# One of four weight-block sums in the downward stages formed by an adding transfer from GpSimd

## The chip, the cores and the metric

The kernel runs on one core of a Trainium2 chip. The metric is the device time of one execution in microseconds. The time before is the median of three runs. One more execution was taken by the hardware profiler; all rows of a profile come from such a single execution.

## The reference

One layer of a streaming encoder on `x` (1024 tokens of 1024 values, float32), with weights in float32. Two SwiGLU feed-forward blocks stand around a mixer of two attentions:

```python
h = modulate(x, norm_g[l, 0], mod[:, 0, 0], mod[:, 0, 1])
x = x + 0.5 * mod[:, 0, 2][:, None, :] * swiglu(h, ffn1_w1[l], ffn1_w3[l], ffn1_w2[l])
h = modulate(x, norm_g[l, 1], mod[:, 1, 0], mod[:, 1, 1])
y = hybrid_mixer(h, w_in[l], ...)
x = x + mod[:, 1, 2][:, None, :] * y
h = modulate(x, norm_g[l, 2], mod[:, 2, 0], mod[:, 2, 1])
x = x + 0.5 * mod[:, 2, 2][:, None, :] * swiglu(h, ffn2_w1[l], ffn2_w3[l], ffn2_w2[l])
```

`swiglu(h, w1, w3, w2)` is `(silu(h @ w1) * (h @ w3)) @ w2` with 2816 inner columns. The last product, by `w2`, is a downward stage; there are two of them, one in each feed-forward block.

## The kernel before

**Precision.** Each float32 operand of a product is split into a high half (`wh`, ScalarE's copy into a rounded format) and a low half (`wl`, VectorE's `src - wh`). A product is three matmuls: high by high, high by low, low by high (`mm3`).

**The downward stage** (class `Down`). `w2` has 22 blocks of 128 rows by 1024 columns. The stage is a 2 x 2 block product, made with seven products instead of eight (Strassen's scheme in Winograd's form). For each of the 11 pairs `q`, the four 128 x 512 blocks of the weight are `a11` and `a12` (block `q`, left and right half) and `a21` and `a22` (block `q + 11`, left and right half). Four sums of blocks are formed, each by one VectorE operation for each `q`: `s3` (`a11 = a11 - a21`), `s2` (`s2 = a22 - a11`), `s1` (`a21 = a21 + a22`) and `s4` (`a12 = a12 - s2`). `ORDER` names the seven products: `a11`, then `a12`, `s2`, the new `a11`, `a22`, the new `a21` and the new `a12`, each by its combination of the hidden values (`g`, which the upward stage has written to `d_g` in HBM). A product `p` runs over the 11 values of `q`; a step (`p`, `q`) splits one weight block and one `g` tile and issues 12 matmuls into four PSUM banks. After the 11 steps, `out` adds the four banks to the output tiles `xc` (and to `u`).

**Where the work waits.** The split tiles `wh` and `wl` come from a ring of 8 each (class `Halves`), so the splits of at most four steps are in being at a time. Raw tiles (`a`, `g`, `xc` and others) come from pools of 128 x 512 tiles. SyncE issues all loads and stores, in one queue; `Down.loads` asks for the tiles of a step six steps ahead.

**The order** is not that of the code. Class `Plan` collects the operations of a long stretch as tasks and places them by a list schedule: it has a guess of the length of each operation (`length`), of when a result can be read (`end`), of a transfer on the wire (`wire`), and of a port that VectorE and GpSimd share (`t.port`). Of the tasks that are ready on each engine it takes the earliest, within a window of 200. It then issues all in that order, and every engine executes its own list in order. Line 358 of `before.py` issues all planned operations, so nearly all rows of the profile carry L358, and the tiles' names tell them apart: `a<-a` is `s3` or `s1`, `s<-a` is `s2`, `a<-a,s` is `s4`, `wl<-a,wh` a low half of a weight block.

**Around it.** GpSimd does little: in the first stage the sums of squares (`nacc`) and some low halves (`wl<-...` of other shapes), in the second nothing. In the first stage the loads for the downward stage start at 443.0 us while the last upward products run; its own matmuls run from about 479 to 699 us. In the second stage the loads start at 2003.6 us, and the kernel ends at 2266.0 us.

Of the kernel before, what the change touches and what calls it, by code (L numbers as in the profile page):

```python
# [16 lines left out]
ALU = mybir.AluOpType  # L17
# [8 lines left out]
H = 512  # L26
# [29 lines left out]
class View:  # L56
# [53 lines left out]
    def real(self):  # L110
        t = self.tile.real()
        for name, a, kw in self.ops:
            t = t[a[0]] if name == "__getitem__" else getattr(t, name)(*a, **kw)
        return t
# [48 lines left out]
class Plan:  # L163
# [18 lines left out]
    def take(self, engine, op, a, kw):  # L182
        if not self.on:
            return getattr(getattr(self.tc.nc, engine), op)(*map(real, a), **{n: real(v) for n, v in kw.items()})
        t = Task(len(self.tasks), engine, op, a, kw)
        t.rank = t.i + self.behind
        self.tasks.append(t)
        writes = [v for v in (a[0], kw.get("accum_out")) if isinstance(v, View)]
        reads = [v for v in list(a[1:]) + [w for n, w in kw.items() if n != "accum_out"] if isinstance(v, View)]
        before = set()  # L190
        for views, write in ((reads, False), (writes, True)):
            for v in views:
                r = v.region()
                for r2, j, w2 in v.tile.log:
                    if (write or w2) and j != t.i and all(p < q2 and p2 < q for (p, q), (p2, q2) in zip(r, r2)):
                        before.add(j)
        for views, write in ((reads, False), (writes, True)):
            for v in views:
                if write and not v.ops:
                    v.tile.log = []  # L200
                v.tile.log.append((v.region(), t.i, write))
        t.ready = max([getattr(v.tile, "written", 0.0) for v in reads] + [0.0])
        tiles = {id(v.tile): v.tile for v in reads + writes + self.wanted}
        self.wanted = []
        for x in tiles.values():
            if x.t is None and x.first is None:
                t.new.append(x)
                x.first = t.i
            elif x.t is None:
                before.add(x.first)  # L210
            x.uses += 1
        t.tiles = list(tiles.values())
        t.written = [v.tile for v in writes]
        for j in before:
            self.tasks[j].after.append(t)
        t.left = len(before)
        out = writes[0] if writes else a[0]
        shape = list(out.shape)
        t.n = int(np.prod(shape[1:]))
        if op == "tensor_reduce":  # L220
            t.n = int(np.prod(a[1].shape[1:]))
        t.bytes = 4 * int(np.prod(shape))
        t.port = engine in ("vector", "gpsimd") and "accum_out" not in kw and not any(
            v.tile.pool.space == PSUM for v in reads + writes)
        if engine == "tensor":
            m = a[2] if op == "matmul" else a[1]
            t.exact = m.tile.dt in (F32R, BF16) or any(o[0] == "bitcast" and F32R in o[1] for o in m.ops)
# [18 lines left out]
    def length(self, t, e):  # L246
        if e == "tensor":
            if t.exact:
                return max(0.08, t.n / 2250.0)
            if t.op == "transpose":  # L250
                return t.n / 860.0
            return max(0.24, t.n / 500.0)
        more = "accum_out" in t.kw
        if e == "scalar":
            return 0.1 + t.n / 1200.0 + (0.3 if more else 0.12 if any(isinstance(t.kw.get(x), View) for x in ("bias", "scale")) else 0.0)
        if e == "vector":
            if t.op == "tensor_tensor_scan":
                return 0.1 + t.n / 450.0
            return max(0.2, 0.08 + t.n / 960.0 + (0.18 if more else 0.06 if t.op == "scalar_tensor_tensor" else 0.0))
        if e == "gpsimd":  # L260
            return 0.1 + t.n / (900.0 if t.op == "tensor_scalar" else 440.0)
        return 0.35

    def flush(self, keep=()):
# [8 lines left out]
        def release(t):  # L273
            insort(waiting[t.engine], t, key=lambda u: u.rank)
# [10 lines left out]
        def slot(t):  # L285

            when, need = 0.0, {}
            for x in t.new:
                if x.kw.get("tag"):
                    need.setdefault(x.key, []).append(x)  # L290
            if need and t.rank > low + self.window:
                return None
            for s, xs in need.items():
                if xs[0].kw["bufs"] == 1 and news[s][0] != t.i:
                    return None
                got = sorted(self.slots(xs[0]))
                if len(got) < len(xs) + (0 if news[s][0] == t.i else min(self.spare, xs[0].kw["bufs"] // 4)):
                    return None
                when = max(when, got[len(xs) - 1][0])
            return when  # L300

        todo = sorted(tasks, key=lambda t: t.rank)
        while len(order) < len(tasks):
            best = None
            while todo[0].placed:
                todo.pop(0)
            low = todo[0].rank
            for e in self.ENGINES:
                w = waiting[e][:60]
                pick, ahead = None, 0.0  # L310
                for t in w:
                    room = slot(t) if t.new else 0.0
                    if room is None:
                        continue
                    s = max(t.ready, room, free[e])
                    if t.port:
                        s = max(s, self.port["gpsimd" if e == "vector" else "vector"])
                    if pick is None or s < pick[0] - 0.05:
                        pick = (s, t, e)
                if pick and (best is None or pick[0] < best[0]):  # L320
                    best = pick
            assert best, "no task can be placed: " + str([(t.engine, t.op, [x.kw for x in t.new]) for w in waiting.values() for t in w][:8])
            s, t, e = best
            d = self.length(t, e)
            end = s + d + 0.12
            if t.port:
                self.port[e] = s + d
            free[e] = s + d
            if e == "sync":
                self.wire = max(self.wire, s + 1.3) + t.bytes / 345e3  # L330
                end = self.wire + 0.7
                free[e] = max(free[e], self.wire - 5.0)
            t.placed = True
            order.append((s, len(order), t, e, d))
            waiting[e].remove(t)
            for x in t.new:
                if x.kw.get("tag"):
                    news[x.key].remove(t.i)
                    x.slot = min(self.slots(x))
                    self.slots(x).remove(x.slot)  # L340
                    x.slot = x.slot[1]
            for x in t.written:
                x.written = max(getattr(x, "written", 0.0), end)
            for x in t.tiles:
                x.uses -= 1
                x.end = max(getattr(x, "end", 0.0), end)
                if not x.uses and x.slot is not None:
                    self.slots(x).append((x.end, x.slot))
                    self.kept.pop(id(x), None)
            for u in t.after:  # L350
                u.left -= 1
                u.ready = max(u.ready, s + d if u.engine == e and e != "sync" else end)
                if not u.left:
                    release(u)
# [152 lines left out]
def t512(k, dt=F32, name="t", home="c"):  # L507

    p, tag, n = k.homes[home]
    return p.tile([128, H], dt, tag=tag, name=name, bufs=n)  # L510
# [824 lines left out]
PAIRS = NF // 2  # L1335
# [232 lines left out]
class Down:  # L1568
# [34 lines left out]
    def sum(self, n, q):  # L1603
        a, nc = {m: t[q] for m, t in self.a.items()}, self.k.nc
        if n == "s3":
            self.any.tensor_sub(a["a11"], a["a11"], a["a21"])
        elif n == "s2":
            t = self.a["s2"][q] = t512(self.k, name="s2")
            self.any.tensor_sub(t, a["a22"], a["a11"])
        elif n == "s1":  # L1610
            self.any.tensor_add(a["a21"], a["a21"], a["a22"])
        elif n == "s4":
            self.any.tensor_sub(a["a12"], a["a12"], a["s2"])

# [668 lines left out]
```

## Time and profile before

| what | value |
|---|---|
| median of 3 runs | 2268.83 us (2267.1 to 2270.32) |
| the profiled execution | 2267.75 us, of which span 2266.0 us |
| mean granted TensorE clock | 0.986 |
| TensorE (PE) busy | 2179.2 us, 96% |
| VectorE (DVE) busy | 1803.8 us, 80% |
| ScalarE (ACT) busy | 1102.1 us, 49% |
| GpSimd (POOL) busy | 296.2 us, 13% |
| DMA, SyncE's queue | 313.89 MB, 41.5% of the span of 16 engines |

Times in the profile are microseconds from the start of the span. A row of a timeline gives start, length, engine, line, operation, result and operands; in brackets stands how long the engine was idle before it and what ended that. A row of a table of groups gives the number of operations and min/median/max of their length in nanoseconds. A row of waits gives the sum, the number of times and the longest.

### The profile page before, as it was taken

The numbers are of one execution on the slowest core, as the hardware profiler recorded it, in microseconds if no ns is written. First come the engines' busy times: TensorE is split into PE (matmuls) and PEld (weight loads), VectorE is DVE, ScalarE is ACT, GpSimd is POOL, SyncE is SP. The second block draws the span as 40 slices with busy tenths as digits, with TensorE's granted clock in tenths as the row PEclk, the third lists the DMA queues.
The fourth block names the chain that finished last, engine by engine and source line by source line (L and its number), as shares of the span: only waits on it lengthen the run. The fifth ranks groups of instructions, "written<-read, shape, count | busy, mean of one in ns | idle before, by whom it ended". The sixth has DMA issues, their size and how long they took to land.

```text
span 2266.0 us, 31234 instructions
## 1 busy us (share of the span) xinstructions
PE 2179.2 (96%) x10508; PEld 1801.7 (80%) x10508; DVE 1803.8 (80%) x3377; ACT 1102.1 (49%) x1996; POOL 296.2 (13%) x269
## 2 busy tenths in 40 slices
PE   7999999999997999998999999799999999999999
PEld 5777888788886989996778787687888888888887
DVE  7998987879685488888688877668898877769765
ACT  5432232344463476787687777423443333334443
POOL 0000000000042113223555433000000000000000
PEclk9999999999998999999999999999999999999999
DMA  9234454495323313333333210767223442258520
GB/s 331 85 113 163 166 173 130 157 355 199 89 92 130 99 49 126 123 120 125 110 106 101 66 44 20 272 227 263 96 80 127 135 132 96 93 186 313 166 77 38
DMA packets 187421, 315.89 MB, mean 139 GB/s; under 512 B 27366, under 2 KB 51942, under 8 KB 187260
## 3 DMA queue, kind: packets, MB, share of 16 engines
q1 hardware_dynamic: 187260, 313.89, 41.5%
q8 instruction: 83, 1.36, 0.3%
q14 instruction: 78, 0.64, 0.1%
HBM read 237.53 MB, written 76.28 MB: 138 GB/s over the span
## 4 chain that ended last, share of the span: by engine, by line
PE 46%; DVE 2%; ACT 2%; DMA 2%; issue 1%; SPq 0%; ACTq 0%; DVEq 0%; POOL 0%
PE b L358 35%; PE py L358 6%; PE pt L358 3%; PE p L358 2%; DMA wr<-in_w_g 1%; ACT pth L358 0%; DVE macc L358 0%; ACT pr L358 0%; DVE ptl L358 0%; ACT kst L358 0%; DMA h<-d_y 0%; DVE qs L358 0%; ACT yt L358 0%; DMA xb<-d_x 0%; DVE kst L358 0%
## 5 line engine op out<-in xcount | busy, mean ns | idle before, releaser
L358 PE MATMUL b<-h,wh 128*128 128x512 f32 x2720 | 855.7, 396 | 10.2 <-ACT wh L358 5.1
L358 PEld LDWEIGHTS b<-h,wh 128*128 128x128 f32 x2720 | 511.9, 189 | 136.0 <-ACT wh L358 9.2
L358 PE MATMUL b<-h,wl 128*128 128x512 f32 x1360 | 533.8, 395 | 1.8 <-DVE wl L358 1.8
L358 ACT ACTIVATE wh<-wr 128x512 fp32r<-128x512 f32 (+2 forms) x368 | 245.5, 676 | 468.9 <-PE b L358 337.2
L358 PEld LDWEIGHTS b<-h,wl 128*128 128x128 f32 x1360 | 256.2, 188 | 63.9 <-DVE wl L358 3.6
L358 DVE TENSOR_TENSOR z<-b,z 128x512 f32<-128x512 f32 x308 | 207.2, 684 | 75.2 <-PE b L358 74.0
L358 PE MATMUL b<-wl,wh 128*128 128x512 f32 x616 | 240.0, 390 | 2.2 <-DVE wl L358 2.2
L358 PE MATMUL b<-wh,wl 128*128 128x512 f32 x616 | 239.7, 389 | 0.0
L358 PE MATMUL b<-wh 128*128 128x512 f32 x616 | 238.5, 390 | 0.7 <-DVE nt L358 0.7
L358 DVE TENSOR_TENSOR wl<-wr,wh 128x512 fp32r<-128x512 f32 x312 | 206.7, 683 | 33.3 <-ACT wh L358 33.2
L358 PE MATMUL pj<-wh,h 128*128 128x384 f32 (+1 forms) x768 | 181.6, 322 | 0.5 <-ACT wh L358 0.4
L358 ACT ACTIVATE wh<-a 128x512 fp32r<-128x512 f32 x132 | 83.4, 631 | 195.0 <-PE b L358 182.5
L358 DVE TENSOR_TENSOR wl<-a,wh 128x512 fp32r<-128x512 f32 x132 | 94.9, 719 | 78.4 <-ACT wh L358 78.4
L358 POOL TENSOR_TENSOR wl<-wr,wh 128x1024 fp32r<-128x1024 f32 (+2 forms) x56 | 119.8, 2145 | 265.0 <-ACT wh L358 258.1
L358 PEld LDWEIGHTS b<-wl,wh 128*128 128x128 f32 x616 | 115.6, 188 | 27.3 <-DVE wl L358 3.5
L358 PEld LDWEIGHTS b<-wh 128*128 128x128 f32 x616 | 115.6, 188 | 25.3 <-issue 1.1
L358 PEld LDWEIGHTS pj<-wh,h 128*128 128x128 f32 x768 | 134.1, 191 | 2.0 <-ACT wh L358 0.9
L358 PEld LDWEIGHTS b<-wh,wl 128*128 128x128 f32 x616 | 115.6, 188 | 24.2
L358 DVE TENSOR_TENSOR z<-z 128x512 f32<-128x512 f32 x176 | 119.4, 690 | 11.2 <-DVE z L358 0.9
L358 PE MATMUL pj<-wl,h 128*128 128x384 f32 (+1 forms) x384 | 123.6, 322 | 0.7 <-POOL wl L358 0.7
L358 POOL TENSOR_SCALAR pr<-pr,mn 128x128 f32<-128x128 f32 (+7 forms) x128 | 101.1, 804 | 154.0 <-DVE mn L358 137.7
L358 DVE TENSOR_TENSOR wl<-g,wh 128x512 fp32r<-128x512 f32 x154 | 112.9, 733 | 0.0
(284 smaller groups left out, 3701.4 us busy)
## 6 DMA issues: line engine op xcount, KB each, us to landing
d_g<-z SPq DMA_DIRECT2D x154, 256.0 KB
g<-d_g SPq DMA_DIRECT2D x154, 256.0 KB
mraw<-in_ada_w SPq DMA_DIRECT2D x144, 256.0 KB
wr<-in_w13a SPq DMA_DIRECT2D x112, 256.0 KB
wr<-in_w13b SPq DMA_DIRECT2D x88, 256.0 KB
wr<-in_w_g SPq DMA_DIRECT2D x32, 512.0 KB
a<-in_w2a SPq DMA_DIRECT2D x44, 256.0 KB
a<-in_w2b SPq DMA_DIRECT2D x44, 256.0 KB
```

The costliest lines, as they stand in the source:

```text
L358: getattr(getattr(self.tc.nc, e), t.op)(*map(real, t.a), **{n: real(v) for n, v in t.kw.items()})
```

## The change

The sum `s1` is no longer an operation of VectorE on two tiles that are already loaded. GpSimd issues a transfer that reads the block `a22` from the weights in HBM once more and adds it to the tile `a21` in place (`accum_op`). SyncE still loads `a22`, which other products use. The planner is told of the new kind of task: it does not take the shared port, it takes GpSimd 1.0 us, and its result is there 3.0 us later. Both downward stages use the class, so there are 22 such transfers of 128 rows of 2 KB.

```diff
-        t.port = engine in ("vector", "gpsimd") and "accum_out" not in kw and not any(
+        t.port = engine in ("vector", "gpsimd") and op != "dma_start" and "accum_out" not in kw and not any(
...
         if e == "gpsimd":
+            if t.op == "dma_start":
+                return 1.0
             return 0.1 + t.n / (900.0 if t.op == "tensor_scalar" else 440.0)
...
             d = self.length(t, e)
-            end = s + d + 0.12
+            end = s + d + (0.12 if t.op != "dma_start" else 3.0)
...
         elif n == "s1":
-            self.any.tensor_add(a["a21"], a["a21"], a["a22"])
+            nc.gpsimd.dma_start(a["a21"], self.w2[q + PAIRS][:, H:2 * H], accum_op=ALU.add)
```

The transfer depends on the subtraction `s3` of the same `q`, which reads `a21`, and no longer on the landing of the tile `a22`.

## The prediction

> **What bounds the kernel now.** I read the page's busy table, its chain that ended last and its costliest groups first, then the waits of TensorE in the two downward stages, then the table of windows over the loading part of each, and last VectorE's timeline there.
>
> ```profile
> span 2266.0 us, 31234 instructions
> ...
> PE 2179.2 (96%) x10508; PEld 1801.7 (80%) x10508; DVE 1803.8 (80%) x3377; ACT 1102.1 (49%) x1996; POOL 296.2 (13%) x269
> ...
> PE 46%; DVE 2%; ACT 2%; DMA 2%; issue 1%; SPq 0%; ACTq 0%; DVEq 0%; POOL 0%
> ```
>
> TensorE is busy for 96% of the span, and the chain names it for 46% against 2% for VectorE. Off this kernel only those VectorE operations can take time that TensorE waits for. So the waits of TensorE inside the two stages come next, first stage (440 to 700 us) and second (2000 to 2266 us):
>
> ```profile
> PE b L358 <- DVE wl L358: 1.3, 2, 1.0
> PE b L358 <- DVE nt L358: 0.7, 1, 0.7
> ```
>
> ```profile
> PE b L358 <- DVE wl L358: 1.0, 1, 1.0
> ```
>
> In both stages together TensorE waits 3.0 us for anything, 2.3 of it for the low halves that VectorE makes (`wl`). That is the whole prize. The windows show what else is full there (columns: PE, PEld, DVE, ACT, POOL busy with counts, TensorE clock, DMA share, GB/s):
>
> ```profile
> 470.00:480.00 10.00, 10.00 (x45) 8.05 (x44) 7.66 (x14) 3.79 (x6) 0.00 (x0) 1.00 1.05 398
> 480.00:490.00 10.00, 10.00 (x46) 8.28 (x45) 9.44 (x15) 3.61 (x7) 0.00 (x0) 1.00 0.75 245
> 490.00:500.00 10.00, 10.00 (x46) 8.04 (x45) 7.21 (x12) 4.95 (x9) 0.00 (x0) 1.00 1.05 390
> 500.00:510.00 10.00, 10.00 (x46) 8.29 (x45) 8.05 (x15) 5.56 (x11) 0.00 (x0) 1.00 1.03 361
> 510.00:520.00 10.00, 10.00 (x46) 8.04 (x45) 10.00 (x17) 4.99 (x10) 0.00 (x0) 1.00 0.48 175
> 2070.00:2080.00 10.00, 10.00 (x46) 8.28 (x45) 8.73 (x16) 5.11 (x10) 0.00 (x0) 1.00 1.05 381
> ```
>
> TensorE never pauses, VectorE has a quarter of its time or less to spare, GpSimd does nothing, and the DMA engines are full (share 1.0) from 490 to 510 and in the second stage while the weights come in. The change takes work from an engine off the path and gives it to the one resource that is full here.
>
> **The change, part by part.**
>
> *VectorE loses 22 additions.* `a21 += a22` is half of this group (the other half is `a11 - a21`, which stays):
>
> ```profile
> L358 DVE TENSOR_TENSOR a<-a x44: 681/684/694, 470.6 to 2092.3; 128x512 f32<-128x512 f32 x44
> L358 DVE TENSOR_TENSOR a<-a x22: 681/684/694, 470.6 to 526.9; 128x512 f32<-128x512 f32 x22
> ```
>
> 22 x 0.684 = 15.0 us of VectorE go, 7.5 in each stage, all of it before 526.9 and 2092.3. TensorE's waits for VectorE lie elsewhere; the longer one of the first stage ends here:
>
> ```profile
> 605.12 1.41 DVE L358 SCALAR_TENSOR_TENSOR xc<-u,G,xc 128x512 f32<-128x512 f32 x2
> 606.45 0.68 DVE L358 TENSOR_TENSOR wl<-g,wh 128x512 fp32r<-128x512 f32 x1
> 607.05 0.68 DVE L358 TENSOR_TENSOR wl<-a,wh 128x512 fp32r<-128x512 f32 x1
> ```
>
> They come after the burst in which the fourth product is added to the outputs (`out`, p == 3), 80 us after the last removed addition. So I price the removal at 0 and not at the 2.3 us that are its upper bound. What hides it is TensorE itself; if that cover were gone the gain would be at most those 15.0 us.
>
> *The order of the rest.* Built, the changed kernel has the same order on TensorE, ScalarE and SyncE. On VectorE the `a12 - s2` subtractions move a few places forward into the holes; on GpSimd 11 transfers stand ahead of the `nacc` sums of the first stage and 11 at the end of the queue. The sums of squares wait for ScalarE until 540.5 us, so GpSimd's queue is free:
>
> ```profile
> 540.50 4.70 POOL L358 TENSOR_TENSOR nacc<-nacc,nsq 128x512 f32<-128x512 f32 x3 [372.66 <-ACT nsq L358]
> ```
>
> Each transfer waits for the subtraction that reads `a21` (the last, in stage 1, starts at 500.38, shown below), and nothing is queued behind it before 540.5. Its result is read by the split of `a21` for the sixth product. A step of a product is 12 matmuls at 10.00/45 = 0.222 us, so 2.67 us, a product of 11 steps some 29 us; the sixth begins five products, about 147 us, after the first. ScalarE and VectorE, which now wait for these transfers there, find them landed over 100 us before. The same holds for the few loads on SyncE's queue into tiles that held `a21`. Cost 0; without that cover it would be one landing per stage.
>
> *22 transfers are added.* Each fetches a second time the 256 KB that SyncE has to load anyway for `a22`:
>
> ```profile
> L358 SPq DMA_DIRECT2D a<-in_w2a x44: 327/376/598, 443.0 to 520.9; - x44
> ...
> a<-in_w2a SPq DMA_DIRECT2D x44, 256.0 KB
> ```
>
> The trace has no transfer that adds. From below: a plain load at the 390 GB/s of the full window takes 262,144 B / 390 = 0.67 us of all DMA engines. From above: source read, destination read and write one after the other, 2.0 us. I take two reads, 1.34 us, since it must read both. The Trainium skill (Collectives: The Full Stack, "The bandwidth ceiling: the fold count and why AG ≠ RS ≠ AR") says that the addition in a DMA engine costs no time, but that the second source read halves the rate; by that page the transfer costs twice a plain one, by the load row alone once, and no run here shows it yet.
>
> Who waits for the DMA engines? In the first stage VectorE does, in order, with splits behind it:
>
> ```profile
> 489.06 0.68 DVE L358 TENSOR_TENSOR a<-a 128x512 f32<-128x512 f32 x1
> 491.73 0.68 DVE L358 TENSOR_TENSOR a<-a 128x512 f32<-128x512 f32 x1
> 494.45 0.68 DVE L358 TENSOR_TENSOR a<-a 128x512 f32<-128x512 f32 x1
> 495.87 0.69 DVE L358 TENSOR_TENSOR a<-a 128x512 f32<-128x512 f32 x1 [0.73 <-DMA a<-in_w2a]
> 496.48 0.68 DVE L358 TENSOR_TENSOR wl<-a,wh 128x512 fp32r<-128x512 f32 x1
> 497.90 0.69 DVE L358 TENSOR_TENSOR a<-a 128x512 f32<-128x512 f32 x1
> 500.38 0.69 DVE L358 TENSOR_TENSOR a<-a 128x512 f32<-128x512 f32 x1
> ```
>
> The subtraction at 495.87 starts when its `a21` lands: here the loads come just in time, and each subtraction now releases a transfer that takes DMA time from the next loads. The first three transfers fall into the slack of 480 to 490 (a quarter of 10 us free). Seven (released by the 4th to the 10th subtraction) run ahead of the last `a21`: at 0.67 us they delay it by 4.7 us, at 1.34 by 9.4, at 2.0 by 14. The cover: the ring of 8 split tiles holds 4 steps, so VectorE is up to 3 steps = 8.0 us ahead of TensorE. TensorE's wait is therefore 0, **1.4** or 6.0 us. A subtraction that is late also releases its own transfer later, so these do not run away.
>
> In the second stage the same subtractions wait for no DMA but for ScalarE, which waits for TensorE:
>
> ```profile
> 2070.86 0.69 DVE L358 TENSOR_TENSOR wl<-a,wh 128x512 fp32r<-128x512 f32 x1 [0.82 <-ACT wh L358]
> 2072.07 0.69 DVE L358 TENSOR_TENSOR a<-a 128x512 f32<-128x512 f32 x1
> 2072.68 0.68 DVE L358 TENSOR_TENSOR s<-a 128x512 f32<-128x512 f32 x1
> ```
>
> The 11 transfers are spread from 2033 to 2075, and what they delay first is the `a22` behind `s<-a`. The load that the first stage waited for at 495.87 is issued in the first of these lines, this one in the second:
>
> ```profile
> 491.21 1.08 SPq L358 DMA_DIRECT2D a<-in_w2a  x2
> ...
> 2056.98 1.10 SPq L358 DMA_DIRECT2D a<-in_w2b  x2
> ```
>
> From 491.21 to 495.87 a load takes 4.7 us in the full window; from 2056.98 to its use at 2072.68 there are 15.7, so 11 to spare, and with the ring's 8 it is 19, against at most 11 x 1.34 = 14.7: 0. At 2.0 us it is 22 against 19: 3 us.
>
> **The sum** against the profiled execution's own 2267.75 us (span 2266.0 and 1.75 around it): -0 + 1.4 + 0 = 2269.2. The median of the runs shown, 2268.83, is 1.1 above that execution, so for a median I give **2270.2 us**; that is within 0.2% (4.5 us), about what a measurement of this kernel can tell from no change.
>
> **The rivals.**
>
> *The loads starve (slower).* Place: first the subtractions at 495 to 501, then `s<-a` at 2072. Price per transfer: from 12.5/7 = 1.8 us on, stage 1 alone costs over 4.5 us. At 2.0 us the two stages cost 6.0 + 3 = 9, so 2278; at 3 us, 7 x 3 - 8 = 13 and 11 x 3 - 19 = 14, so 2296 before the feedback. For it: DMA share 1.05 in the stages, a subtraction that already waits for its load. Against: no row shows a transfer slower than its bytes. An unknown price, so 0.36.
>
> *GpSimd blocks VectorE while it writes descriptors (mostly slower).* GpSimd's own sum beside VectorE did this:
>
> ```profile
> 540.98 1.36 DVE L358 TENSOR_TENSOR wl<-g,wh 128x512 fp32r<-128x512 f32 x1
> 542.26 1.78 DVE L358 TENSOR_TENSOR wl<-s,wh 128x512 fp32r<-128x512 f32 x1
> 543.96 1.77 DVE L358 TENSOR_TENSOR wl<-g,wh 128x512 fp32r<-128x512 f32 x1
> ```
>
> An operation of 0.68 became 1.78. If each of the 8 transfers of 485 to 501 stretched two operations by 1.1 us, VectorE would need 17.6 us more, has about 5 us idle and 2 of removed additions there, and the ring covers 8: TensorE waits some 3 us a stage, 2276. Against: those operations met a GpSimd that read SBUF data, a transfer's issue does not. The Trainium skill (SBUF — State Buffer, "Who interferes with whom") says just this: a VectorE operation with two SBUF inputs contends with a GpSimd instruction that reads SBUF, not with one that only writes; the 1.78 us row agrees with its first half, and by its second half this rival costs 0. 0.10.
>
> *VectorE's relief reaches TensorE (faster).* All 2.3 us of TensorE's waits for `wl` go and the transfers are hidden: 2266.5, still within 0.2%. Against: the distance of 80 us. 0.08, of which I leave 0.05 to a gain over 0.2% by a way that I do not see.
>
> *The additions stay, or the transfers are not issued*: the built order excludes it, 0.
>
> **How the numbers follow.** Forecast 0.46 (same, 0 to +4.5 us). Slower: 0.36 from starved loads and 0.08 of the 0.10 of the blocked VectorE, 0.44. Same: 0.46 + 0.02 + 0.03 = 0.51. Faster 0.05. The range starts at 2265, below the 2266.5 of the gain by the spread of the runs before, and ends at 2290, between 2.0 and 3 us a transfer; the forecast's own range is 2267 to 2273.
>
> **What would show it.** Right: 22 fewer `a<-a` operations (VectorE -15 us), 22 transfers on a queue of their own, which fill the DMA share of 480 to 490 from 0.75 to about 1.0 and raise that of 510 to 520 from 0.48, `a<-a` around 496 to 505 waiting for `a<-in_w2a` by several us, and TensorE's waits for `wl` near 500 at 1 to 2 us. Wrong: TensorE idle by more than 4 us between 490 and 530 or 2070 and 2100 (transfers slower than 1.8 us), operations of 1.7 us on VectorE beside the transfers (blocked), a sixth product that waits for the transfers, or a wait near 607 that is gone with no new one.

## The result, and the profile after

The changed kernel takes 2277.8 us (median of 6 runs, 2275.59 to 2281.15) against 2268.97 us of the kernel before in the same comparison (2263.55 to 2270.38). The ratio is 1.0045, 95% interval 1.0035 to 1.0055: slower, by 8.8 us between the medians and some 10 by the ratio. That lies inside the wide range of the forecast, but not where its likeliest case stood. The profiled execution has a span of 2275.1 us, 9.1 more than before.

The page after, in its busy table and its DMA queues (packets, MB, share of 16 engines):

```profile
PE 2181.1 (96%) x10508; PEld 1801.1 (79%) x10508; DVE 1792.4 (79%) x3355; ACT 1101.7 (48%) x1996; POOL 314.7 (14%) x291
...
q1 hardware_dynamic: 187260, 313.89, 40.6%
q0 software_dynamic: 3168, 5.77, 1.4%
```

VectorE has 22 operations fewer, as planned. The transfers have a queue of their own, and it is dear for its bytes: 1.4% of 2275.1 us for 22 transfers is some 1.4 us of all 16 DMA engines for each (the times of its packets in the trace add up to 1.41). The bytes counted there are those of the source alone.

TensorE's waits, first stage and second, which were 2.0 and 1.0 us in all:

```profile
PE b L360 <- DVE wl L360: 7.2, 3, 5.0
PE b L360 <- DVE nt L360: 0.7, 1, 0.7
```

```profile
PE b L360 <- DVE wl L360: 3.6, 4, 1.6
```

They grew by 5.9 and 2.6 us. What the stages lost in all shows on one group of matmuls, by the start of its first and its last one in a stage: before and after in the first stage, then before and after in the second.

```profile
L358 PE MATMUL b<-wh x308: 388/389/478, 479.0 to 698.2; 128*128 128x512 f32 x154
L360 PE MATMUL b<-wh x308: 388/389/628, 480.1 to 707.7; 128*128 128x512 f32 x154
```

```profile
L358 PE MATMUL b<-wh x308: 388/389/391, 2051.2 to 2261.2; 128*128 128x512 f32 x154
L360 PE MATMUL b<-wh x308: 388/389/398, 2056.6 to 2270.2; 128*128 128x512 f32 x154
```

That is 219.2 against 227.6 us and 210.0 against 213.6: 8.4 and 3.6 us more. Who held VectorE up? Its own waits from 460 to 530 us, and from 2030 to 2105 us (sum, times, longest):

```profile
DVE a L360 <- DMA a<-in_w2a: 8.3, 5, 3.3
DVE mod L360 <- DMA mcol<-d_row: 7.2, 1, 7.2
```

```profile
DVE s L360 <- DMA a<-in_w2b: 6.1, 2, 5.1
DVE a L360 <- DMA a<-in_w2b: 4.9, 2, 4.3
```

In the first of these stretches the kernel before had hardly any such wait, and in the second none for a load:

```profile
DVE a L358 <- DMA a<-in_w2a: 0.7, 1, 0.7
DVE mod L358 <- DMA mcol<-d_row: 0.2, 1, 0.2
```

The wait of `mod` is one operation on 128 x 4 values. VectorE's timeline shows where it stands:

```profile
498.97 0.69 DVE L360 TENSOR_TENSOR a<-a 128x512 f32<-128x512 f32 x1 [3.28 <-DMA a<-in_w2a]
502.23 0.69 DVE L360 TENSOR_TENSOR a<-a 128x512 f32<-128x512 f32 x1 [2.56 <-DMA a<-in_w2a]
...
507.44 0.69 DVE L360 TENSOR_TENSOR a<-a 128x512 f32<-128x512 f32 x1 [1.31 <-DMA a<-in_w2a]
...
518.37 0.16 DVE L360 TENSOR_TENSOR mod<-mcol,ada_b 128x4 f32<-128x4 f32 x1 [7.23 <-DMA mcol<-d_row]
```

`mcol` is a column of the modulation vector: a row of 2 KB is stored to HBM (`d_row`) and read back as a column. That is two transfers in series, and both stand in SyncE's queue among the weights. VectorE executes in order, so four additions to the outputs and the low halves between and behind them stood for 7.2 us behind a tile that nobody needed soon (the run with the column moved, below, shows that it could wait). The windows show what TensorE did (PE, PEld, DVE, ACT, POOL busy, clock, DMA share, GB/s):

```profile
517.00:519.00 2.00, 0.00 (x0) 0.00 (x0) 0.60 (x3) 0.13 (x1) 0.00 (x0) 0.98 1.06 377
519.00:521.00 2.00, 0.00 (x0) 0.00 (x0) 2.00 (x4) 0.00 (x0) 0.00 (x0) 0.50 1.05 387
521.00:523.00 2.00, 1.63 (x4) 1.34 (x5) 2.00 (x4) 0.00 (x0) 0.00 (x0) 0.50 1.05 385
523.00:525.00 2.00, 2.00 (x7) 1.52 (x6) 1.99 (x4) 0.00 (x0) 0.00 (x0) 0.50 1.05 385
525.00:527.00 2.00, 2.00 (x9) 1.28 (x8) 1.98 (x4) 1.02 (x2) 0.00 (x0) 0.82 0.33 119
```

When VectorE's wait begins, at 511.14, TensorE has 5.3 us of work left; it runs dry at 516.4. It idles until 521.4: 2.0 us until `mcol` has landed, and 3.0 more while VectorE does two tiny operations and three additions before the next low half. The granted clock is 0.50 from 519 until after 525. The matmuls that run in that time lose some 2 us more, which no row of waits counts. Of the 8.4 us of the stage, 5.0 are this wait and 2 the clock. About 1 more is a longer wait for a low half at 670 us (1.2 us against 0.2), whose cause no run settles. The two stages lost 12.0 us and the span only 9.1, so the rest of this execution was 2.9 us shorter than in the profiled execution before. Stages that the change doesn't touch scatter by that much.

### The profile page after: what moved, and what is told of

Read it like the earlier page. It is cut to its first block, busy times and chain, and to the rows that moved or that the text cites. A ratio compares the mean times of both kernels' runs of the same rounds, so it can differ in the third digit from the quotient of the medians.

```text
span 2275.1 us, 31288 instructions
## 1 busy us (share of the span) xinstructions
PE 2181.1 (96%) x10508; PEld 1801.1 (79%) x10508; DVE 1792.4 (79%) x3355; ACT 1101.7 (48%) x1996; POOL 314.7 (14%) x291
## 3 DMA queue, kind: packets, MB, share of 16 engines
q0 software_dynamic: 3168, 5.77, 1.4%
## 4 chain that ended last, share of the span: by engine, by line
PE 45%; DMA 2%; DVE 2%; ACT 2%; issue 1%; SPq 0%; ACTq 0%; DVEq 0%; POOL 0%; POOLq 0%
PE b L360 34%; PE py L360 6%; PE pt L360 3%; PE p L360 2%; DMA g<-d_g 1%; DMA a<-in_w2b 1%; ACT pth L360 0%; ACT pr L360 0%; DVE xc L360 0%; DVE ptl L360 0%; DMA wr<-in_w_g 0%; DVE qs L360 0%; DMA wr<-in_wbr 0%; ACT kst L360 0%; ACT yt L360 0%
```

## The experiments

Theory: an adding transfer takes twice the DMA time of a plain one, and takes it from loads for which VectorE waits in order; TensorE feels only what the ring of split tiles doesn't cover. Each run has 9 or 11 executions, measured beside the kernel before. All edits are to the changed kernel. The rows of each run come from one profiled execution of it. Since whole executions scatter by several us, the table at the end gives the length of the two stages in each.

**The same transfers later.** In `Down.run`, with a dependency of the 11 transfers on the copy:

```diff
+            if p == 3:
+                k.nc.hold = len(k.nc.tasks)
+                k.nc.gpsimd.tensor_copy(k.c.tile([128, 1], F32, tag="hold", name="hold", bufs=2), self.u[3][:, 0:1])
```

> All 22 adding transfers are kept, but GpSimd first copies one column of a tile that the third product writes, so the 11 transfers of a stage go out together when the third product is done (about 570 and 2150 us); the order on the other four engines is that of the changed kernel. Theory (the transfers take the DMA engines' time from loads for which VectorE waits in order): there the DMA share was 0.3 to 0.5 and every load is far ahead, so TensorE's waits for VectorE's low halves fall from 7.2 and 3.6 us back to about 1.3 and 1.0, and the time to 2269 us (2266 to 2272). Rival (issuing 22 transfers, or having them in flight, costs VectorE or GpSimd time wherever it happens): the time stays at 2276 to 2280 us.

Measured: 2270.08 us, ratio 1.0008 (0.9999 to 1.0017). The loss can no longer be told from none, with all 22 transfers. GpSimd's timeline and the windows of the first stage:

```profile
574.14 0.19 POOL L363 COPY hold<-u 128x1 f32<-128x1 f32 x1 [28.05 <-DVE u L363]
574.72 8.02 POOL L363 DMA_DIRECT2D a<-in_w2a  x9 [0.39 <-issue]
```

```profile
580.00:590.00 10.00, 10.00 (x46) 8.29 (x45) 4.61 (x8) 3.81 (x7) 4.44 (x6) 1.00 1.07 248
590.00:600.00 10.00, 10.00 (x46) 8.29 (x45) 5.37 (x9) 4.27 (x8) 0.00 (x0) 1.00 1.07 254
```

The transfers fill the DMA engines here too (share 1.07), but VectorE waits for no load from 570 to 615 us, and TensorE has its 46 matmuls in each 10 us. Its waits are those of before:

```profile
PE b L363 <- DVE wl L363: 1.2, 2, 1.0
```

**Plain copies instead of additions.**

```diff
-            nc.gpsimd.dma_start(a["a21"], self.w2[q + PAIRS][:, H:2 * H], accum_op=ALU.add)
+            nc.gpsimd.dma_start(a["a21"], self.w2[q + PAIRS][:, H:2 * H])
```

> The same 22 transfers at the same places, but as plain copies: a22 is written over a21 and the addition is left out, so the sixth product works on other numbers. Theory (the price is DMA time, 1.41 us for an adding transfer by its 176 ns packets, 0.67 for a plain one by 84 ns): seven transfers delay the last a21 by 4.7 us instead of 9.9, which the ring covers, so TensorE's waits fall to 1 to 3 us in stage 1 and about 1 in stage 2, and the time to 2270 to 2272 us. Rival (fetching the block a second time at all, or issuing from GpSimd, is what costs): as the changed kernel, 2276 to 2280.

Measured: 2268.29 us, ratio 1.0005 (0.9996 to 1.0013), even a little less than expected. The queue on the page and TensorE's waits in the first stage:

```profile
q0 software_dynamic: 1760, 5.77, 0.7%
```

```profile
PE b L360 <- DVE wl L360: 2.8, 3, 1.2
```

The same 5.77 MB take 0.7% instead of 1.4%, some 0.7 us for each transfer (0.68 by the packets). So the second fetch alone nearly fits under the ring's cover: VectorE still stood 4.6 us for `a21` and 4.8 us for `mcol`, and only 1.5 us of it reached TensorE.

**The same issues with few bytes.**

```diff
-            nc.gpsimd.dma_start(a["a21"], self.w2[q + PAIRS][:, H:2 * H], accum_op=ALU.add)
+            nc.gpsimd.dma_start(a["a21"][:, 0:16], self.w2[q + PAIRS][:, H:H + 16], accum_op=ALU.add)
```

> The same 22 adding transfers at the same places with 16 of the 512 columns: 128 rows of 64 bytes, 8 KB instead of 256 KB; the other 496 columns of the sum are left out. Theory: DMA time nearly gone, waits as in the kernel before, 2269 us (2266 to 2271). Rival (descriptors, GpSimd's 0.85 us per issue, VectorE held up by the descriptor writes): 22 issues and as many rows as before, so 2275 to 2280.

Measured: 2267.92 us, ratio 0.9998 (0.9990 to 1.0007). GpSimd is as long at it as with whole blocks, first here and then in the changed kernel:

```profile
493.26 0.85 POOL L360 DMA_DIRECT2D a<-in_w2a  x1 [1.25 <-PE b L360]
```

```profile
491.89 0.85 POOL L360 DMA_DIRECT2D a<-in_w2a  x1 [1.72 <-DVE a L360]
```

So the issue costs the kernel nothing that can be measured. In the changed kernel VectorE's `wl<-g,wh` at 492.29, within that second issue, took its usual 0.68 us.

**The modulation column later.** After the plan of the first stage two operations move down VectorE's list:

```diff
+            for o in vec[n:n + 2]:
+                self.trace.remove(o)
+            n = self.trace.index(vec[n + 26])
...
```

> The changed kernel, but the two tiny VectorE operations that read the modulation column mcol just after the last a11 - a21 of the first stage stand some 24 VectorE operations later; nothing else moves. Theory (VectorE stood 8.3 us for late a21 blocks, which the ring covers, and TensorE's 5.0 us came only with the 7.2 us in which VectorE stood for mcol, whose 2 KB round trip had queued behind the same full DMA engines): TensorE's wait of 5.0 us shrinks to under 1.5, the drop of the granted clock after it goes too, time 2271 us (2269 to 2273). Rival (the late a21 blocks alone empty the ring): the wait stays at 4 to 5 us, 2276 to 2279.

Measured: 2272.69 us, ratio 1.0022 (1.0012 to 1.0032), near the upper end of the expectation. TensorE's wait of 5.0 us is gone from the first stage, although VectorE waits nearly as long for the late blocks (8.3 us in the changed kernel), and still for the column, only later:

```profile
PE b L369 <- DVE wl L369: 1.3, 2, 1.0
```

```profile
DVE a L369 <- DMA a<-in_w2a: 7.3, 4, 3.5
...
DVE mod L369 <- DMA mcol<-d_row: 3.7, 1, 3.7
```

So the ring covers 7.3 us of late blocks, and it covers 3.7 us of waiting when it has had time to fill again. What it did not cover was the two in close succession. The column's wait on a full ring, without late blocks, was not run. What is left of the loss is in the second stage:

```profile
2080.00:2082.00 2.00, 0.37 (x2) 0.00 (x0) 1.79 (x3) 1.62 (x4) 0.00 (x0) 1.00 1.11 264
2082.00:2084.00 2.00, 1.84 (x7) 1.46 (x8) 0.98 (x3) 0.00 (x0) 0.00 (x0) 0.84 1.05 396
2084.00:2086.00 2.00, 2.00 (x6) 1.58 (x5) 2.00 (x4) 0.13 (x1) 0.00 (x0) 0.50 1.05 404
2086.00:2088.00 2.00, 2.00 (x8) 1.60 (x7) 2.00 (x5) 1.02 (x2) 0.00 (x0) 0.80 1.05 385
```

There TensorE waits 1.8 us, and from about 2083.4 on it again has the half clock, for 3.4 us.

**No sum at all.**

```diff
-            nc.gpsimd.dma_start(a["a21"], self.w2[q + PAIRS][:, H:2 * H], accum_op=ALU.add)
+            pass
```

> The sum a21 + a22 is left out altogether, neither added by VectorE nor by a transfer, so the sixth product works on other numbers; the order on TensorE, ScalarE and SyncE is that of the changed kernel. Theory (15 us of VectorE's work off the path are worth nothing to TensorE): 2268 us (2265.5 to 2270), TensorE's waits for VectorE's low halves again about 1.3 and 1.0 us. Rival (the relief is worth something that the transfers ate): 2265 or less, and then the transfers cost that much more.

Measured: 2268.54 us, ratio 1.0008 (0.9999 to 1.0017). TensorE's waits are 1.3 and 1.0 us again. That is the ceiling of the whole idea: 15 us of VectorE's work gone for nothing in return are worth no time that can be measured.

**Half of the transfers.**

```diff
+            if q % 2:
+                self.any.tensor_add(a["a21"], a["a21"], a["a22"])
+            else:
```

> Only the even of the 11 sums of a stage are formed by a transfer (6), the odd ones (5) stay on VectorE. Theory (delays add up with DMA time until the ring of four steps is used up, and only the rest costs): 6 x 1.41 = 8.5 us of DMA time a stage, about that of 11 plain copies (7.4), so hardly any wait: 2269 to 2271 us. Rival (each transfer costs its share of the 9 us): half of it, 2272 to 2274 us.

Measured: 2268.71 us, ratio 1.0010 (1.0000 to 1.0020), just below the expected band; one of its eleven executions took 2277.49 us, which nothing kept explains. Half the transfers cost about a fifth of the loss (between none and 0.44 of it by the interval), not half: the loss grows faster than the DMA time. TensorE's waits in the first stage are 1.9 us, 0.6 above before.

**The second stage alone.**

```diff
+            if self.s != 2:
+                self.any.tensor_add(a["a21"], a["a21"], a["a22"])
+            else:
```

> The transfers in the second downward stage alone; the first keeps VectorE's sums. Theory (2 to 3 us of waits for late a21 and a22 there, and 1 to 1.5 us of a granted clock of 0.5 behind them): 2271.5 us (2270 to 2273). Rival (all 9 us come from the mcol wait of the first stage): 2268 to 2269.5 us.

Measured: 2273.19 us, ratio 1.0022 (1.0014 to 1.0031), just above the expected band. The profile shows the waits of the second stage again:

```profile
PE b L360 <- DVE wl L360: 3.4, 4, 1.3
```

That is 2.4 us above before; in this execution no half clock followed. The interval says 3.2 to 7.0 us in all, and the stage's matmuls took 3.4 us longer, which lies in it. The profiled execution is the shortest of the eleven, 2267.83 us, no longer than the kernel before in its profile. Its second stage began 3.6 us earlier than there, at 2047.6 instead of 2051.2 us, so its total hides what the stage lost.

**The two stages in all runs.** From the first to the last start of the matmuls `b<-wh` of a stage, in the profiled execution of each run:

| run | first stage, us | second stage, us |
|---|---|---|
| before | 219.2 | 210.0 |
| changed kernel | 227.6 | 213.6 |
| transfers later | 219.1 | 210.0 |
| plain copies | 221.1 | 210.1 |
| few bytes | 219.2 | 210.1 |
| column later | 219.3 | 213.8 |
| no sum | 219.3 | 210.1 |
| half of the transfers | 220.2 | 210.1 |
| second stage alone | 219.3 | 213.4 |

A stage that loses nothing has the same length within 0.2 us in every run. The second stage loses 3.4 to 3.8 us with 11 adding transfers and nothing with 6 or with plain copies. The first loses 1.0 us with 6 adding transfers, 1.9 with plain copies, 8.4 with 11, and nothing with 11 when the column stands later.

No version was faster than the kernel before.

## Why the prediction was right or wrong

*The removal at 0*: right. The run without any sum has a ratio of 1.0008, and TensorE's waits of 1.3 and 1.0 us stayed.

*The order, GpSimd's queue, the readers of `a21`*: right. No split waited for a transfer, and the issues of 0.85 us cost nothing that could be measured.

*The transfer at 1.34 us*: right. Some 1.4 us, twice the 0.7 us of the plain copy on the same queue. The Trainium skill (Collectives: The Full Stack, "The bandwidth ceiling: the fold count and why AG ≠ RS ≠ AR") has the rate halved by the second source read; the factor of 2 agrees with it, while its reason no run here shows.

*The delay of the late blocks in the first stage*: the mechanism was right, the size too large. 9.4 us were forecast for the last `a21`. Its subtraction started at 507.44 instead of 500.38, 7.1 us later, of which 1.1 are the later start of the stage. Two of the seven transfers that I counted ahead of it landed only after it (510.1 and 512.2 us against 507.4, by the times in the trace at which a transfer raises its semaphore), which may be the reason. TensorE's 1.4 us from this term were 0 in the run with the column moved.

*Who waits for the DMA engines*: this is the step that failed in the first stage. I listed the subtractions and `s<-a`, and looked for what is behind them, but not for what else on VectorE's list waits for a transfer just then. `mod<-mcol` did, 11 us after the last delayed subtraction, with two transfers in series. Its 7.2 us came on a ring that the late blocks had drawn down to 5.3 us of cover. Forecast were 1.4 us of waiting, and 5.9 more than before were measured. With the column moved they are gone: without this wait just behind them, the late blocks cost nothing.

*The second stage at 0*: wrong, because the spare time was misread. I put 11 us of spare before `s<-a`, from the load issued at 2056.98 and used at 2072.68. In the changed kernel the wait of this `s<-a` ends with the landing of another load, and that load's place in SyncE's list, which is the same in both kernels, gives its issue before (first row) and after (second row):

```profile
2066.10 0.33 SPq L358 DMA_DIRECT2D a<-in_w2b  x1
2078.94 0.33 SPq L360 DMA_DIRECT2D a<-in_w2b  x1
...
2086.62 0.69 DVE L360 TENSOR_TENSOR s<-a 128x512 f32<-128x512 f32 x1 [5.11 <-DMA a<-in_w2b]
```

By its semaphore it landed at 2071.51 before, 1.2 us ahead of its use, and at 2086.60 after. So there were 1.2 us to spare, not 11, and the cover was some 9 us against the forecast 14.7: by the same sum 5.5 us of waiting, where 2.6 came. The 4.7 us for a load came from the wrong row too: the `a21` that 495.87 waited for was issued at 489.61, 6.2 us before. Much of the lateness arose before the issue. This load was issued 12.8 us later in a stage that began 5.4 later. SyncE, in order as well, waited longer for the landing of earlier transfers (2010 to 2095 us, before and after):

```profile
SPq L358 <- DMA g<-d_g: 4.2, 14, 0.4
SPq L360 <- DMA g<-d_g: 14.7, 25, 1.7
```

VectorE stood 4.9 us for late `a21` and 6.1 for `s<-a`, 11.0 us in 18, with little room for the ring to fill in between. No run separates these two.

*The range*: the measured time lies in it, but not by the sum, which gave 2270.2 and its own range of 2267 to 2273. The range reached to 2290 for the rival of starved loads. That this rival names 2278 for 2.0 us a transfer is luck: the price was 1.4, and the stages lost 8.4 and 3.6 us instead of its 6.0 and 3.

*What was not in the sum*: the clock after a wait. Some 2 us in the first stage came from a granted clock of 0.50.

*GpSimd blocks VectorE*: refuted by the transfers of 64 bytes a row, 0.9998. The rule of the Trainium skill (SBUF — State Buffer, "Who interferes with whom"), by which VectorE's operations on two tiles don't contend with a GpSimd that only writes, agrees with the 0.68 us beside the issues.

*The rival of starved loads*: its mechanism was right, and in the second stage its place; in the first the subtractions that it names cost TensorE nothing by themselves. I gave it 0.36 because I hung it on a price from 1.8 us on, and it came true at 1.4: what I had wrong was a wait left out in the first stage and the spare time in the second.

## What to carry to other kernels

A transfer that adds took the DMA engines twice the time of a plain one here, and in a stretch where they are full that time comes out of the loads queued behind it. Before work is moved to the DMA engines, go through the in-order list of every engine for all operations that wait for any transfer in that stretch, the tiny ones of an unrelated stage too, and add their delays up against one cover, since a ring of buffers that one wait has drawn down does not cover the next one in full. Take the spare time of a load from its own landing, not from a row of the same name. And if the result is needed late, make the transfer wait for a quiet stretch: the same 22 transfers, some 80 to 100 us later, cost nothing that could be measured.

## What the runs showed of the hardware

The granted clock of TensorE was 0.50 after an idle time of 5.0 us, and after one of 1.8 us in the run with the column moved, for 6.8 and 3.4 us by the windows above. After waits of up to 1.6 us in the second stage of the changed kernel it stayed at 1.00, and so it did after the 1.0 us at 607 in the kernel before:

```profile
606.00:608.00 2.00, 0.97 (x5) 0.68 (x5) 2.00 (x4) 0.22 (x1) 0.00 (x0) 1.00 0.27 104
608.00:610.00 2.00, 2.00 (x10) 1.68 (x9) 2.00 (x4) 0.89 (x2) 0.00 (x0) 1.00 0.49 137
```

The Trainium skill (TensorE: Matmul & The Clock Gate, "Part 1: The HAM clock gate (the "warmup" mystery)") has half the clock after an idle window of some 3.4 us; the 5.0 us agree, the 1.8 us are shorter than that. The estimate of what it cost, half of the time in which matmuls ran at 0.50, is some 2 us on top of the 5.0 and some 1.7 on top of the 1.8.

An adding transfer of 128 rows of 2 KB occupied the 16 DMA engines for some 1.4 us and a plain one from the same queue for some 0.7 us. An adding transfer took GpSimd 0.85 us to issue, with rows of 2 KB and of 64 bytes alike, a plain one 0.54 us.
